# A streaming encoder step on one core: one weight sum moved between projections, a shorter sample softmax, other buffers for late gating, and a different order of the last split

## The chip, the cores and the metric

The kernel runs on one core of one Trainium2 chip. The metric is device time in microseconds (us) for one execution, as the median of the runs. The kernel before took 2306.07 us (three runs, 2305.02 to 2309.39). A measurement of this kernel can tell about 0.2% from no change.

## The reference, cut to what matters

One layer of a streaming encoder is applied to a prompt of 2048 tokens and to a batch of 8 samples with 16 tokens each, 2176 tokens in 17 tiles of 128. All arithmetic is float32.

```python
def trunk_layer(x, ...):                      # d_model 1024
    qm, km, vm, om, ip, fp, qa, ka, va = split_in(x @ w_in)         # in-projection
    hm = sigmoid(om) * head_norm(mlstm_chunkwise(qm, km, vm, ...))  # 4 heads x 128
    ha = swa(rope(qa), rope(ka), va, attn_sinks)                    # 8 query heads x 64, 2 kv heads
    mix = concat([hm, ha]) @ w_out                                  # out-projection
    h = layer_norm(alpha * x + mix)
    u = h @ w_up                                                    # 1024 -> 2 x 2816
    c = b_conv + sum(ext(u)[j:j + T] * w_conv[j] for j in range(3)) # causal depthwise
    a, g = split(c)
    return layer_norm(alpha * h + (silu(g) * a) @ w_down)           # 2816 -> 1024
```

The attention of the samples sees a cache of 128 keys and 16 new ones. Its softmax has a sink for each head, which counts in the maximum and in the sum:

```python
mx = maximum(max(s), sink)
p = exp(s - mx)
p = p / (sum(p) + exp(sink - mx))
```

## The kernel before

**Matrix products.** Every large product is float32 accuracy from reduced pieces: an operand is split into a high part (a cast on ScalarE, line 218) and a rest (a subtraction on VectorE, line 219), and three matmuls make one product (`mm3`, line 223, and the loops at 713, 1883 and 2090). The in-projection, the up-projection and the down-projection also use a scheme with seven products of half-size blocks in place of eight, for which sums of weight blocks and sums of token blocks are made on VectorE. The products are numbered 1 to 7 in the code (`s`).

**Buffers of weights.** Raw weights arrive by DMA in the seven buffers of tag `wraw` (`WR = 7`), 128 x 1024 float32 each, which all stages share. Their splits go to a ring of eight halves, later ten (tags `wlo`, `whi`, `wex`).

**Stages.** TensorE's order is the order of the program; the other engines' queues are put in order by the scheduler at compile time, which moves an operation ahead as soon as its inputs and its buffer allow.

1. In-projection (`i_dense`): four blocks of four prompt tiles (the samples go with block 0), five groups `g` of output columns, seven products each. Woven into it are chains for each tile (`t_sample`, `m_chain`, `a_chain`): the sample's mLSTM and attention (`swa_sample`, line 1480 on) and then the prompt's, tile by tile. A chain puts its matmuls between the dense ones at places that a plan with estimated costs sets.
2. Out-projection (`o_block`): five blocks of tiles, two halves `hf` of the output columns each, with the remaining chains woven in, and the first layer norm.
3. ConvFFN up (`f_ups`): three blocks of tokens (768, 768 and 640), 22 pairs of value and gate tiles each. `f_evict` copies TensorE's sums out, `f_after` does the convolution for the value (after product 3) and the gate (after product 4). For blocks 1 and 2, `f_gate` makes silu(gate) * value at once and stores it to `zf`. For block 0 the convolved tiles are stored to `zc` instead, and loaded back and gated later: 18 of them within block 1, four within block 2 (lines 1953 to 1959). The convolved tiles of the current pair and those that are loaded back share the two buffers of tag `cc`.
4. ConvFFN down (`f_downs`): three blocks, seven products, six units of weights each, with the second layer norm. `d_weights` loads and splits a unit; `pending` holds the norm steps of finished tiles (statistics, line 2128; two passes, lines 2130 and 2132), and `step` issues the next step of up to two of them. For the last block each step is put behind the latest split of weights on VectorE (`issue_after(self.low)`).

**Sums for the down-projection.** `d_sums` (line 849 on) makes ready the sums of `w_down` that stage 4 reads from `zt`, one pair of weight tiles k (of eleven) at a time. It has three steps: two loads of 512 KB, four subtractions of 128 x 512 on VectorE, two stores of 512 KB. Three of the eleven are made in the in-projection (line 691), in the single buffers `xr1` and `xr3`, and eight in the out-projection (line 1616), in two `wraw` buffers.

**From the out-projection to the ConvFFN.** The normed tiles come back from `zh` as `hst` (lines 1723 and 1725, on ScalarE's DMA queue), are transposed on TensorE (line 1707) between the matmuls of the last block of the out-projection, and the first ConvFFN weights (`wv`, `wg`, lines 1780 and 1782) are loaded meanwhile. The input of that last block comes as `xraw` from `zmix` and is split on ScalarE and VectorE (lines 902 to 907).

**Sample softmax.** In `swa_sample`, for each half of the batch: the maximum and a copy of the scores (lines 1511, 1512), the larger of the scaled maximum and the sink (1513), sink minus maximum (1514), its exponential (1515), the negated maximum (1516), four exponentials with sums (1518), sum and reciprocal (1519, 1520), and the scaling on GpSimd (1521). TensorE then transposes the result (1527, 1528).

Of the kernel before, what the change touches and what calls it, by code (L numbers as in the profile page):

```python
# [8 lines left out]
F32 = mybir.dt.float32  # L9
# [5 lines left out]
P = 128  # L15
# [190 lines left out]
class Prog:  # L206
# [384 lines left out]
    def i_dense(self):  # L591
# [36 lines left out]
        for item in self.items:  # L628
            if after:

                after[0] -= 1
                if after[0] == 3:
                    self.logs_of(after[1] - 1)
                if after[0] < 0:
                    self.i_done = after[1]
                    after = None
            self.chains.hold = item[0] == "t" and item[1] > 0
            if item[0] == "t":
                _, b, ti, e = item
                if ("g", e, 3) not in self.wu:  # L640
                    self.advance()
                if b not in self.gates:
                    self.gates[b] = self.tp.tile([P, 5, 8], F32, name="gates", tag="gates", bufs=2)
                if b == 0 and ti == 1:
                    for h in range(2):
                        for i in range(2):
                            yield from self.i_direct(b, i, e, self.ib[i * 2], (h,))
                    self.i_keys(b, 0, self.ib[0])
                    self.i_keys(b, 1, self.ib[2])
                    self.advance()  # L650
                    continue
                ps = self.bank([P, 512], "pg") if ti == 4 else self.ib[ti % 2 * 2]
                yield from self.i_direct(b, ti, e, ps)
                self.i_keys(b, ti, ps)
                if ti == 3 and b or ti == 4:
                    self.release(4)
                    self.x_steps(b, 4)
                    if b:
                        self.x_steps(b, 5)
                self.advance()  # L660
                continue
            _, b, g, s = item
            if item not in self.wu:
                self.advance()
            yield from self.i_product(b, g, s)
            del self.wu[item]
            self.release(2)
            if self.trans and s != 4:
                self.i_transposes()
            with self.tc.high_priority():  # L670
                behind = self.i_after(b, g, s)
            if (b, g, s) == (0, 0, 7):
                self.t_setup()
            if (g, s) == (last, 4):
                after = [8, b + 1]
            if g == last and b + 1 < nb:
                if s == 7:
                    for i in (0, 2):
                        self.rope_load(IBLOCKS[b + 1][i], 2)
                for x in passages[b > 0].get(s, ()):  # L680
                    if x == "load":
                        self.spare = True
                        self.x_load(b + 1, 1, 2, 3, 4)
                    else:
                        self.x_steps(b + 1, x)
            if g == last and b + 1 == nb and s in (7, 5, 2, 3):
                self.x_pair(0, (7, 5, 2, 3).index(s))
            with self.tc.issue_after(behind) if behind and b == 0 else nullcontext():
                self.advance()

            if (b, g) in ((nb - 2, 1), (nb - 1, 0), (nb - 1, 2)):

                steps = (6, 5, 3)
                if s in steps:
                    self.d_sums(sums, steps.index(s))
                    sums += s == steps[2]
# [244 lines left out]
    def t_setup(self):  # L941
        nc, a, tp = self.nc, self.a, self.tp

        def ld(n):
            t = self.one("k_" + n, list(a[n].shape))
            nc.sync.dma_start(t, a[n])
            return t
        nc.sync.dma_start(self.ident, a["ident"])
        self.gb = ld("gb")
        self.mcau = ld("mcau")  # L950
        self.mswa = ld("mswa")
        self.seg = ld("seg")
        self.sink = ld("sink")
        self.sinkx = ld("sinkx")
        self.m0 = ld("m0")
        self.nsink = self.one("nsink", [P, 8])
        nc.vector.tensor_scalar_mul(self.nsink, self.sink, -1.0)
        nc.vector.tensor_scalar_mul(self.sink, self.sink, 8.0)
        self.gm = ld("gm")
        nc.vector.tensor_scalar_mul(self.gm, self.gm, 0.5)  # L960

        raw = self.work("kw", [36, MH])
        nc.sync.dma_start(raw, a["sel"])
        self.sel = self.one("sel", [36, MH], F32R)
        nc.vector.tensor_copy(self.sel, raw)
        self.hl = [self.one(f"hl{i}", [36, P], F32R) for i in range(2)]
        self.ay = [self.one(f"ay{i}", [36, P]) for i in range(2)]
        for i in range(2):
            nc.vector.memset(self.ay[i], 0.0)
            nc.vector.tensor_copy(self.hl[i], self.ay[i])  # L970
        self.kh, self.kl = [self.one(n, [P, RING, P], F32R) for n in ("kringh", "kringl")]
        self.kv = {}
        self.C = self.work("C", [P, MH, 129], bufs=2)
        nc.vector.memset(self.C, 0.0)

        self.M = self.row("M")
        self.mc = self.M[:, P:]
        nc.vector.memset(self.mc, 0.0)
# [501 lines left out]
    def swa_sample(self, load, kvc):  # L1480
# [11 lines left out]
        mix = self.work("mixa", [P, 4, P])  # L1492
        NK = P + DS
        HB = DB // 2
        sk = self.sinkx.to_broadcast([P, HB])
        for half in range(2):
            bs = slice(half * HB, half * HB + HB)
            kc, vc = kvc
# [4 lines left out]
            for b0 in (0, 2):  # L1503
# [6 lines left out]
                        nc.tensor.matmul(ps[rs, i, P:], qs[rs, b], ks[rs, b * DS:(b + 1) * DS], start=True, stop=True)  # L1510
                V.tensor_reduce(mx[:, b0:b0 + 2], ps, axis=AX.X, op=ALU.max)
                V.tensor_copy(sc[:, b0:b0 + 2], ps)
            V.scalar_tensor_tensor(mx, mx, 0.125, sk, op0=ALU.mult, op1=ALU.max)
            V.tensor_sub(es, sk, mx)
            nc.scalar.activation(es, es, AF.Exp)
            V.tensor_scalar_mul(mx, mx, -1.0)
            for b in range(HB):
                nc.scalar.activation(sc[:, b], sc[:, b], AF.Exp, bias=mx[:, b:b + 1], scale=0.125, accum_out=sm[:, b:b + 1])
            V.tensor_add(sm, sm, es)
# [77 lines left out]
    def o_block(self, b):  # L1597
# [7 lines left out]
        for hf in range(2):  # L1605
            c = slice(hf * 512, hf * 512 + 512)
            steps = 0
            for cost, ti, ps in self.group(b, tiles, 8 * b + 4 * hf, hf == 1):
                yield cost
                if ps is None:  # L1610
                    steps += 1
                    if hf and b + 1 < nb and steps == 8 * len(tiles) - 6:
                        self.ynext = [self.o_x(t) for t in OBLOCKS[b + 1][:2]]
                    if steps % 2 == 0 and self.norms and next(self.norms[0], self) is self:
                        del self.norms[0]
                    if self.sums < NK2 and steps in (2, 18, 22):
                        self.d_sums(self.sums, (2, 18, 22).index(steps), True)
                        self.sums += steps == 22
                    continue
                y = outs[ti]  # L1620
                with self.tc.high_priority():
                    nc.vector.scalar_tensor_tensor(y[:, c], ys[ti][:, c], ALPHA, ps, op0=ALU.mult, op1=ALU.add)
                if hf and b == nb - 2 and ti >= len(tiles) - 2:

                    nc.sync.dma_start(self.zh[tiles[ti]], y)
                elif hf and b < nb - 1:
                    self.norms.append(self.norm(y, *self.ln1, self.zh[tiles[ti]]))
# [295 lines left out]
    def f_after(self, b, j, s):  # L1923
# [23 lines left out]
        if b == 0:  # L1947

            nc.sync.dma_start(self.zc[j], c)
            return  # L1950
        self.f_gate(c, b, j, WP, n)

        i = (b - 1) * NFF + j
        i = i if i < 18 else i - 6 if 24 <= i < 28 else None
        if b and i is not None:
            W0 = len(FBLOCKS[0]) * P
            c = self.f3.tile([P, 2, 768], F32, name="cc", tag="cc", bufs=2)[:, :, :W0]
            nc.sync.dma_start(c, self.zc[i])
            self.f_gate(c, 0, i, W0, W0)

    def f_gate(self, c, b, j, WP, n):
        nc, V = self.nc, self.nc.vector
        W = len(FBLOCKS[b]) * P
        th = self.f3.tile([P, 768], F32, name="th", tag="th", bufs=1)[:, :n]
        nc.scalar.activation(th, c[:, 1], AF.Tanh, scale=0.5)  # L1965
        V.scalar_tensor_tensor(th, th, 1.0, c[:, 1], op0=ALU.add, op1=ALU.mult)  # L1966
        V.tensor_mul(c[:, 0], th, c[:, 0])  # L1967
        nc.sync.dma_start(self.zf[b][j, :, :WP], c[:, 0, :WP])
        if n > WP:
            nc.sync.dma_start(self.zf[b][j, :, WP:].rearrange("p (b l) -> p b l", b=DB),  # L1970
                              c[:, 0, WP:].rearrange("p (b l) -> p b l", b=DB)[:, :, 2:])

# [88 lines left out]
    def f_downs(self):  # L2063
# [78 lines left out]
        for g, (b, s, u) in enumerate(self.dseq):  # L2142
# [41 lines left out]
                self.d_weights()  # L2184
            while self.nt < min(g + 6, len(self.dseq)):
                self.d_tokens()
            if b == nb - 1:
                with self.tc.issue_after(self.low):
                    step()


# [13 lines left out]
```

## Time and profile before

| | before |
|---|---|
| median of three runs | 2306.07 us |
| the profiled execution's own time | 2308.3 us |
| its span, first to last instruction | 2306.5 us |
| mean granted clock of TensorE | 0.998 |
| DVE (VectorE) busy | 1808.6 us, 78% |
| ACT (ScalarE) busy | 1271.4 us, 55% |
| POOL (GpSimd) busy | 273.7 us, 12% |
| DMA | 631.30 MB, 274 GB/s on average |

A row of the profile names the engine, the line of the kernel, the operation and its tiles (written<-read). PE is TensorE, PEld its weight loads, SPq the DMA queue of the Sync engine and ACTq that of ScalarE. What stands in square brackets is the idle time of the engine just before, and what ended it. Shares of DMA are of all 16 DMA engines of the core; they may come out slightly above 1.

### The profile page before, as it was taken

To read this page: it belongs to the slowest core of one execution; us is meant where nothing else is said; L and a number is where in the kernel's file an instruction comes from. 1 tells how busy PE (TensorE), PEld (TensorE's weight loads), DVE (VectorE), ACT (ScalarE), POOL (GpSimd) and SP (SyncE) were. 2 spreads that over 40 slices of the span, in tenths; PEclk is the share of its full clock that TensorE was granted. 3 is DMA by queue.
4 is the path that set the end of the run, shared out by engine and by line. 5 is a ranking of instruction groups with operands and counts; after the bars stand their busy time and mean duration, and the time that the engine had idled before them with its cause. 6 is when DMAs were issued, how large, how long until landed. Compare 5 with 4: busy or idle time off the path is not lost. (4 is left out here: it accounts for less than half of the span.)

```text
span 2306.5 us, 39717 instructions
## 1 busy us (share of the span) xinstructions
PE 2278.0 (99%) x14293; PEld 2092.2 (91%) x14293; DVE 1808.6 (78%) x3071; ACT 1271.4 (55%) x2373; POOL 273.7 (12%) x509
## 2 busy tenths in 40 slices
PE   9999999999999999999999999999999999999998
PEld 8999999999877777999999999999999978888876
DVE  8787587777688888998778777678766786895987
ACT  5453476776766655555656555555555544444442
POOL 0001001000121110211112100013111200100100
PEclk9999999999999999999999999999999999999999
DMA  7988898899997876898778888978998786757742
GB/s 279 322 306 291 296 315 276 276 305 299 326 327 257 280 246 250 304 325 302 276 277 277 303 302 312 311 255 288 308 299 261 246 297 214 253 172 222 255 155 83
DMA packets 299733, 631.30 MB, mean 274 GB/s; under 512 B 47820, under 2 KB 141072, under 8 KB 299536
## 3 DMA queue, kind: packets, MB, share of 16 engines
q1 hardware_dynamic: 294864, 615.06, 78.2%
q0 software_dynamic: 3520, 10.56, 1.5%
q10 hardware_dynamic: 1152, 3.15, 0.4%
q8 instruction: 113, 1.85, 0.3%
q14 instruction: 84, 0.69, 0.1%
HBM read 457.02 MB, written 171.64 MB: 273 GB/s over the span
## 5 line engine op out<-in xcount | busy, mean ns | idle before, releaser
L1883 PE MATMUL fup<-hh,uw 128*128 128x384 f32 (+1 forms) x1848 | 478.2, 328 | 1.2 <-ACT ua L1904 1.2
L1883 PE MATMUL dps<-hh,uw 128*128 128x384 f32 (+1 forms) x1848 | 477.8, 328 | 0.0
L1883 PEld LDWEIGHTS fup<-hh,uw 128*128 128x128 f32 x1848 | 330.1, 188 | 1.6 <-ACT ua L1904 1.5
L1883 PEld LDWEIGHTS dps<-hh,uw 128*128 128x128 f32 x1848 | 329.9, 188 | 0.0
L1941 DVE SCALAR_TENSOR_TENSOR cc<-u,cw,cc 128x768 f32<-128x768 f32 (+1 forms) x264 | 258.1, 978 | 63.2 <-ACT cc L1939 54.8
L1883 PE MATMUL fup<-hl,uw 128*128 128x384 f32 (+1 forms) x924 | 302.6, 327 | 1.0 <-DVE hl L219 1.0
L1883 PE MATMUL dps<-hl,uw 128*128 128x384 f32 (+1 forms) x924 | 302.4, 327 | 0.0
L713 PE MATMUL dps<-w,oh 128*128 128x256 f32 x1344 | 255.5, 285 | 0.0
L218 ACT CAST uw<-wraw 128x1024 fp32r<-128x1024 f32 x126 | 123.2, 978 | 230.2 <-PE dps L2090 122.2
L219 DVE TENSOR_TENSOR w<-wraw,w 128x1024 fp32r<-128x1024 f32 (+2 forms) x163 | 186.4, 1152 | 67.6 <-ACT w L218 61.6
L713 PEld LDWEIGHTS dps<-w,oh 128*128 128x128 f32 x1344 | 211.6, 189 | 11.1 <-issue 8.1
L218 ACT CAST w<-wraw 128x1024 fp32r<-128x1024 f32 (+2 forms) x163 | 160.0, 991 | 107.1 <-PE dps L713 55.4
L219 DVE TENSOR_TENSOR uw<-wraw,uw 128x1024 fp32r<-128x1024 f32 x126 | 142.2, 1129 | 62.9 <-ACT uw L218 62.0
L713 PE MATMUL dps<-w,ol 128*128 128x256 f32 x672 | 188.3, 280 | 0.0
L2090 PE MATMUL fup<-uw,fu 128*128 128x512 f32 x726 | 173.9, 396 | 1.6 <-ACT fht L2098 1.6
L1883 PEld LDWEIGHTS fup<-hl,uw 128*128 128x128 f32 x924 | 173.5, 188 | 1.7 <-DVE hl L219 1.6
L1883 PEld LDWEIGHTS dps<-hl,uw 128*128 128x128 f32 x924 | 173.5, 188 | 0.0
L713 PE MATMUL dps<-oh,w 128*128 128x256 f32 x896 | 168.0, 282 | 3.9 <-DVE w L219 2.3
L2090 PEld LDWEIGHTS fup<-uw,fu 128*128 128x128 f32 x726 | 136.3, 188 | 34.8 <-ACT fht L2098 2.0
L2090 PE MATMUL dps<-uw,fu 128*128 128x512 f32 x660 | 165.2, 396 | 1.1 <-DVE uw L219 1.1
L1939 ACT ACTIVATE cc<-u,cw 128x768 f32<-128x768 f32 (+1 forms) x132 | 132.1, 1001 | 48.7 <-DVE u L1921 23.4
L2090 PEld LDWEIGHTS dps<-uw,fu 128*128 128x128 f32 x660 | 123.9, 188 | 31.3 <-DVE uw L219 1.5
(318 smaller groups left out, 4574.1 us busy)
## 6 DMA issues: line engine op xcount, KB each, us to landing
uw<-zw SPq DMA_DIRECT2D x176, 512.0 KB, 5.2
zw<-uw SPq DMA_DIRECT2D x88, 512.0 KB, 3.5
w<-zws SPq DMA_DIRECT2D x72, 512.0 KB, 5.8
wv<-wup SPq DMA_DIRECT2D x66, 512.0 KB, 4.7
wraw<-wi SPq DMA_DIRECT2D x65, 512.0 KB, 5.1
wraw<-zt SPq DMA_DIRECT2D x60, 512.0 KB, 4.5
wraw<-wdn SPq DMA_DIRECT2D x45, 512.0 KB, 4.4
wraw<-wo SPq DMA_DIRECT2D x40, 512.0 KB, 5.4
```

The lines of the kernel that those rows point to most:

```text
L218: nc.scalar.copy(hi, src)
L219: return nc.vector.tensor_sub(lo, src, hi.bitcast(F32)).ins
L713: mm(o, l, r, start=s in (1, 7) and c == k == i == 0, stop=k == 3 and i == 2, skip_group_check=True)
L1883: mm(ps, l[:, k], r[:, k], start=s in (1, 7) and k == 0 and i == 0, stop=k == 3 and i == 2, skip_group_check=True)
L1939: S.activation(c[:, v], u[:, 2:2 + n], AF.Identity, bias=w[3], scale=w[2])
L1941: V.scalar_tensor_tensor(c[:, v], u[:, i:i + n], w[i], c[:, v], op0=ALU.mult, op1=ALU.add)
L2090: mm(ps, l[:, k, c], r[:, k], start=s in (1, 4, 7) and u == 0 and k == 0 and i == 0, stop=u == nu - 1 and k == n - 1 and i == 2, skip_grou ...
```

## The change

1. In the in-projection a fourth sum is made, in group 1 of the last block; in the out-projection the condition now allows sums up to the block and half `(nb - 2, 0)` only, so that seven are made there and none in the last half of the block before the last.
2. The sample softmax keeps the negated maximum from the start (`min` of -0.125 times the maximum and the negated sink), and the sink's exponential takes the sink as its bias. Lines 1514 and 1516 go; one operation that negates the sink is added at the setup of the chains.
3. The convolved tiles of block 0 are loaded back into two `wraw` buffers by two DMAs, gate first, and no longer into a `cc` buffer by one.
4. In the down-projection, the norm step that came between the last but one and the last split of weights is not issued there; what is pending is issued after the last unit.

```diff
@@ i_dense
-            if (b, g) in ((nb - 2, 1), (nb - 1, 0), (nb - 1, 2)):
+            if (b, g) in ((nb - 2, 1), (nb - 1, 0), (nb - 1, 1), (nb - 1, 2)):
@@ t_setup
+        self.nsinkx = self.one("nsinkx", [P, 1])
+        nc.vector.tensor_scalar_mul(self.nsinkx, self.sinkx, -1.0)
@@ swa_sample
-        sk = self.sinkx.to_broadcast([P, HB])
+        nsk = self.nsinkx.to_broadcast([P, HB])
...
-            V.scalar_tensor_tensor(mx, mx, 0.125, sk, op0=ALU.mult, op1=ALU.max)
-            V.tensor_sub(es, sk, mx)
-            nc.scalar.activation(es, es, AF.Exp)
-            V.tensor_scalar_mul(mx, mx, -1.0)
+            V.scalar_tensor_tensor(mx, mx, -0.125, nsk, op0=ALU.mult, op1=ALU.min)
+            nc.scalar.activation(es, mx, AF.Exp, bias=self.sinkx)
@@ o_block
-                    if self.sums < NK2 and steps in (2, 18, 22):
+                    if (b, hf) < (nb - 2, 1) and steps in (2, 18, 22):
@@ f_after
-        self.f_gate(c, b, j, WP, n)
+        self.f_gate([c[:, k] for k in range(2)], b, j, WP, n)
...
-            c = self.f3.tile([P, 2, 768], F32, name="cc", tag="cc", bufs=2)[:, :, :W0]
-            nc.sync.dma_start(c, self.zc[i])
+            c = [self.wp.tile([P, 768], F32, name="cz", tag="wraw", bufs=WR)[:, :W0] for _ in range(2)]
+            for k in (1, 0):
+                nc.sync.dma_start(c[k], self.zc[i][:, k])
             self.f_gate(c, 0, i, W0, W0)
@@ f_downs
-            if b == nb - 1:
+            if b == nb - 1 and self.nw != len(self.dseq) - 1:
                 with self.tc.issue_after(self.low):
                     step()
+        while pending:
+            step()
```

In `f_gate` the indices `c[:, 0]` and `c[:, 1]` become `c[0]` and `c[1]`, with the same operations.

More of the change, by code (lines that the diff above doesn't have):

```diff
@@ L1964, in f_gate @@
         th = self.f3.tile([P, 768], F32, name="th", tag="th", bufs=1)[:, :n]
[L1965 to L1968, printed above, removed]
+        nc.scalar.activation(th, c[1], AF.Tanh, scale=0.5)
+        V.scalar_tensor_tensor(th, th, 1.0, c[1], op0=ALU.add, op1=ALU.mult)
+        V.tensor_mul(c[0], th, c[0])
+        nc.sync.dma_start(self.zf[b][j, :, :WP], c[0][:, :WP])
         if n > WP:
             nc.sync.dma_start(self.zf[b][j, :, WP:].rearrange("p (b l) -> p b l", b=DB),
-                              c[:, 0, WP:].rearrange("p (b l) -> p b l", b=DB)[:, :, 2:])
+                              c[0][:, WP:].rearrange("p (b l) -> p b l", b=DB)[:, :, 2:])
     def d_begin(self):
```

## The prediction

> **What bounds the kernel now.** First the page's busy times, then the list of waits of TensorE, longest first (microseconds in all, times, longest).
>
> ```profile
> PE 2278.0 (99%) x14293; PEld 2092.2 (91%) x14293; DVE 1808.6 (78%) x3071; ACT 1271.4 (55%) x2373; POOL 273.7 (12%) x509
> ...
> PE fht L1707 <- DMA hst<-zh: 4.3, 3, 3.1
> PE ppt L1527 <- POOL v L1103: 2.9, 1, 2.9
> ...
> PE fup L2090 <- ACT fht L2098: 1.6, 1, 1.6
> ...
> PE fup L1883 <- ACT ua L1904: 1.2, 1, 1.2
> PE dps L2090 <- DVE uw L219: 1.1, 1, 1.1
> ```
>
> TensorE is busy for 2278.0 of 2306.5 us, and the change takes no matmul away. What it can win are the waits in this list, and four of its parts each stand beside one: the batch's softmax (2.9, the POOL row), the last transposes ahead of the ConvFFN (4.3), the gating (1.2), the last split (1.1). Together these are 9.5 us.
>
> A wait can cost more than its gap. The busy times in windows show the granted clock (third number from the end; the last two are DMA share and GB/s) after the two longest single waits, and after the one of 1.6 us:
>
> ```profile
> 254.00:258.00 4.00, 4.00 (x23) 3.92 (x22) 0.00 (x0) 1.82 (x3) 0.00 (x0) 0.59 0.59 168
> 882.00:886.00 4.00, 4.00 (x17) 3.55 (x18) 2.35 (x2) 1.41 (x3) 0.00 (x0) 0.58 0.11 45
> 1858.00:1860.00 2.00, 1.91 (x8) 1.60 (x9) 1.50 (x2) 2.00 (x5) 0.00 (x0) 1.00 1.04 394
> ```
>
> TensorE counts as busy in both first windows, but at 0.59 and 0.58 of its clock: 4 us times 0.41 or 0.42 is 1.65 us of work lost, twice. After the wait of 1.6 us the clock was 1.00. So I count that a stall that falls below 1.6 us takes 1.65 us of slow clock with it. [...] The trace has the fall behind both stalls.
>
> **The change part by part.** *The batch's softmax.* Its first half in order of time (start, length, engine, line):
>
> ```profile
> 246.67 0.15 DVE L1513 SCALAR_TENSOR_TENSOR amx<-amx,k_sinkx 128x4 f32<-128x4 f32 x1
> ...
> 248.55 1.22 DVE L219 TENSOR_TENSOR w<-wraw,w 128x1024 fp32r<-128x1024 f32 x1
> ...
> 249.69 0.16 DVE L1516 TENSOR_SCALAR amx<-amx 128x4 f32<-128x4 f32 x1
> 249.88 0.41 ACT L1518 ACTIVATE scs<-scs,amx 128x144 f32<-128x144 f32 x1 [1.01 <-DVE amx L1516]
> ...
> 251.61 0.17 DVE L1519 TENSOR_TENSOR asm<-asm,aes 128x4 f32<-128x4 f32 x1 [1.77 <-ACT scs L1518]
> ...
> 252.13 1.15 POOL L1521 TENSOR_TENSOR scs<-scs,asm 128x576 f32<-128x576 f32 x1 [26.37 <-DVE asm L1520]
> ...
> 253.34 0.33 PE L1527 MATMUL ppt<-ident,scs 128*128 128x128 f32 x1 [2.85 <-POOL v L1103]
> ```
>
> The operations of lines 1514 and 1516 go. What counts is not their 0.16 us each but that VectorE does other work ahead of each, the split of 1.22 us among it: ScalarE's exponentials start at 249.88, 3 us after the minimum is there (246.82). Without them the exponentials can start near 247; the four took 1.73 us (249.88 to 251.61), so even behind another operation of ScalarE they are done before VectorE leaves its split at 249.77. The sum of line 1519 then runs there and not at 251.61: 1.9 us earlier, and with it the chain behind it; I take 2.0. The stall falls from 2.85 to about 0.9, and the slow clock goes: **3.6 us**. Bounds: 0 (the schedule keeps the old spacing) and 2.85 + 1.65 = 4.5. The second half has no wait in the list: nothing. The new negated sink is one more operation like that of line 1516, early, where no wait of TensorE is left to lengthen by more than its 0.16 us: nothing.
>
> *One sum less in the out-projection.* Its four subtractions on VectorE delay nobody in the list. Its transfers do (rows of the engines, then two windows):
>
> ```profile
> 849.12 0.33 SPq L865 DMA_DIRECT2D zt<-txy  x1
> ...
> 866.68 0.33 SPq L1780 DMA_DIRECT2D wv<-wup  x1
> ...
> 867.53 0.62 ACT L906 CAST oh<-xraw 128x512 fp32r<-128x512 f32 x1 [2.44 <-DMA xraw<-zmix]
> ...
> 870.67 0.34 ACTq L1725 DMA_DIRECT2D hst<-zh  x1
> ...
> 881.91 1.94 PE L1707 MATMUL fht<-ident,hst 128*128 128x128 f32 x8 [3.09 <-DMA hst<-zh]
> ...
> 850.00:866.00 16.00, 16.00 (x70) 12.14 (x69) 11.12 (x17) 4.87 (x9) 2.90 (x2) 1.00 0.99 332
> 866.00:882.00 16.00, 11.70 (x60) 8.90 (x60) 8.79 (x11) 7.46 (x10) 0.00 (x0) 1.00 1.04 416
> ```
>
> From 850 to 882 the DMA engines are full (shares 0.99 and 1.04). The last load of hst leaves ScalarE's queue at 870.67 and is waited for until 881.91; the loads ahead of it were queued on ScalarE behind casts that themselves waited for transfers, like the one at 867.53. The two stores of the sum, 1.05 MB, are 3.2 us of the full stretch at 332 GB/s and 2.5 at 416. I take 3.0, as they stand in its first half: of 4.3 us of waiting 1.3 stay, under the 1.6 that left the clock alone, so the 1.65 go too: **4.6 us**. Bounds: 0 and 4.3 + 1.65 = 5.9.
>
> *The fourth sum in the in-projection* uses the third one's two single buffers after it (SP's queue, TensorE, one window, one row of the page's issues):
>
> ```profile
> 485.06 0.96 SPq L854 DMA_DIRECT2D txy<-wdn  x1
> ...
> 504.21 0.41 SPq L866 DMA_DIRECT2D zt<-txy  x1
> ...
> 523.27 2.18 SPq L483 DMA_DIRECT2D w<-zws  x3
> ...
> 532.46 0.28 PE L713 MATMUL dps<-w,oh 128*128 128x256 f32 x1
> ...
> 510.00:530.00 20.00, 20.00 (x168) 17.46 (x167) 11.37 (x48) 14.75 (x41) 2.01 (x4) 1.00 1.03 351
> ...
> w<-zws SPq DMA_DIRECT2D x72, 512.0 KB, 5.8
> ```
>
> The third runs from 485 to 504, so the fourth would run from about 509 to 528, and there the DMA engines are full (1.03). The stored half that is issued at 523.27 lands some 5.8 us later, at 529.1; the product that starts at 532.46 has 3.4 us in hand. Loads and stores of one sum are 2.1 MB, at 351 GB/s 6.0 us. If all of that goes ahead of these halves, on SP's queue or in the engines, TensorE waits 2.6 us and with the clock 4.3; if only the loads do, it does not wait. There is no wait of TensorE here to gain. I take a third of the bare wait: **-0.9 us**.
>
> *Later gating in raw buffers.* The 1.25 us, what ScalarE (which issues in order) waited for ahead of it, the same wait over the whole run, one product, and the load of a raw weight:
>
> ```profile
> 1637.35 0.85 ACT L1965 ACTIVATE th<-cc 128x768 f32<-128x768 f32 x1 [4.12 <-DMA cc<-zc]
> ...
> 1641.30 0.93 ACT L1939 ACTIVATE cc<-u,cw 128x656 f32<-128x656 f32 x1 [1.69 <-DMA zf<-cc]
> ...
> 1642.59 0.41 PE L1883 MATMUL fup<-hh,uw 128*128 128x320 f32 x1 [1.25 <-ACT ua L1904]
> ...
> ACT cc L1939 <- DMA zf<-cc: 22.5, 21, 2.0
> ...
> 1664.00 1.76 PE dps L1883 x12
> ...
> wv<-wup SPq DMA_DIRECT2D x66, 512.0 KB, 4.7
> ```
>
> With cc's two buffers kept for the current tile, neither wait is left. In exchange each pair of tiles takes four turns of the seven raw buffers, not two. Taken in turn, a load of wv gets its buffer when the last split of the wg two pairs earlier ends, three products (5.3 us at 1.76) ahead of its own split; the earlier split's own 1.2 us (as long as the one at 248.55) off, 4.1 us are left for a load of 4.7. ScalarE would wait about 0.6 us per pair, where it now waits 22.5 / 21 = 1.1 us for the stores mostly unnoticed. The 22 more DMA issues fall to SP, 0.33 us each like that at 849.12, between loads made long ahead; without that cover they would be 7 us. I take **0.9 us** of the 1.25. Bounds: 1.25, and below nothing the third rival.
>
> *Last split ahead of a norm step.*
>
> ```profile
> 2282.45 2.47 DVE L2130 SCALAR_TENSOR_TENSOR yacc<-yacc,lmv,f_ln_g 128x1024 f32<-128x1024 f32 x2
> ...
> 2284.84 0.68 DVE L219 TENSOR_TENSOR uw<-wraw,uw 128x512 fp32r<-128x512 f32 x1
> ...
> 2285.58 0.74 PE L2090 MATMUL dps<-uw,fu 128*128 128x512 f32 x2 [1.09 <-DVE uw L219]
> ...
> 2298.93 0.69 DVE L2119 SCALAR_TENSOR_TENSOR yacc<-yacc,fht 128x512 f32<-128x512 f32 x1 [1.25 <-PE fht L2090]
> ```
>
> The split would run from 2282.45 to 2283.13, before TensorE asks at 2284.49. The norm steps come 0.68 us later; VectorE still waits for TensorE at 2298.93, so the end moves with TensorE: **1.1 us**. Bound: 0, if another operation slips in.
>
> **The sum:** 3.6 + 4.6 - 0.9 + 0.9 + 1.1 = 9.3 us. The profiled execution took 2308.3 us, 1.8 of them outside its span; it would take 2299.0. It lies 2.2 above the median of the runs, 2306.07, so the median becomes **2296.8**.
>
> **The rivals.**
> 1. *Prefetch takes what the stores free.* The two raw buffers of the sum go to the ConvFFN's first weights: the load at 866.68 comes earlier, and the next pair of loads takes its place beside hst. For: the engines are full up to 882, whoever fills them. Against: the first pair then goes ahead of the full stretch. The hst term is gone: 2306.07 - 4.7 = 2301.4. [...] 0.17.
> 2. *The fourth sum stalls the in-projection* at 532: 4.3 lost and not 0.9 gives 2300.2. For: 3.4 us in hand against 6.0. Against: the third sum moved as much and stalled nobody in the list. 0.10.
> 3. *Slower: the raw ring.* If loads of wv hold ScalarE as long as it was held at 1637 and 1641 (4.12 + 1.69 = 5.8 us) at each of the 22 gates, each costs TensorE 1.25: 27.5 us, less the other parts' 8.4, gives 2325. It decides from a landing of 4.1 + 5.8 = 9.9 us on; the median is 4.7. 0.07.
> 4. *The clock falls although the stalls are short:* 3.3 us stay, 2300.1. 0.06.
> 5. *The change does not do what it says:* VectorE's order keeps the softmax as late as before; 3.6 us stay, 2300.4. 0.05.
> 6. Two of the smaller ones together: about 2305. 0.05.
>
> **How the numbers follow.** The forecast has 0.50. A measurement of this kernel can tell about 0.2%, 4.6 us, from no change: faster is below 2301.5, slower above 2310.7. Faster: 0.47 of the forecast, half of rival 1, most of 2, 4 and 5, in all 0.70. Slower: rival 3, 0.07. Within: the rest, 0.23. The low end takes the upper bounds, 4.5 + 5.9 + 1.25 + 1.1 = 12.75: 2293. The high end takes in rivals 1, 2, 4 and 5 with some spread: 2304; left out are rivals 3 and 6 and the tails.
>
> **What would show it.** In the list of waits: the POOL row of ppt at 1 us or less, hst under 2, no row for ua or for the last uw; a granted clock of 1.00 near 254 and 882; no wait near 532; ScalarE's waits for wv under 1 us each. An unchanged 3 us at hst, or a new wait of TensorE above 1.6 us anywhere, would make the prediction wrong.

## The result, and the profile after

The changed kernel takes 2302.03 us (median of 16 runs, 2299.82 to 2305.87), the kernel before on the same chip 2307.43 (16 runs). The ratio is 0.998, 95% interval 0.9973 to 0.9986: 5.4 us faster, where 9.3 were forecast. The profiled execution took 2301.44 us with a span of 2299.7, 6.8 less than the span before.

From the list of waits of TensorE of the changed kernel:

```profile
PE ppt L1354 <- ACT pth L1355: 2.7, 1, 2.7
...
PE ppt L1527 <- POOL scs L1521: 0.8, 1, 0.8
PE ppt L1354 <- DVE C L1235: 0.8, 1, 0.8
```

The rows for hst, ua and the last uw are gone, and the row of the samples' softmax fell from 2.9 to 0.8. At the top stands a wait that the kernel before did not have: the transposes of line 1354, in the attention chain of the in-projection.

Where the time went can be read from landmarks, because both kernels run the same 14293 matmuls in the same order. These rows are starts of the same TensorE work: the transposes of four chains' gates (pcol, called a to d below), the first product of the ConvFFN (line 1883), and the last products (fht). First the kernel before:

```profile
305.25 0.25 PE L1034 MATMUL pcol<-ident,ay 36*128 36x36 f32 x1
...
484.18 0.25 PE L1034 MATMUL pcol<-ident,ay 36*128 36x36 f32 x1
518.39 0.25 PE L1034 MATMUL pcol<-ident,ay 36*128 36x36 f32 x1
818.96 0.25 PE L1034 MATMUL pcol<-ident,ay 36*128 36x36 f32 x1
903.47 0.34 PE L1883 MATMUL fup<-hh,uw 128*128 128x384 f32 x1
...
2286.16 12.73 PE L2090 MATMUL fht<-uw,fu 128*128 128x512 f32 x54
```

Then the changed kernel:

```profile
301.97 0.25 PE L1036 MATMUL pcol<-ident,ay 36*128 36x36 f32 x1
...
480.98 0.25 PE L1036 MATMUL pcol<-ident,ay 36*128 36x36 f32 x1
520.12 0.25 PE L1036 MATMUL pcol<-ident,ay 36*128 36x36 f32 x1
821.12 0.25 PE L1036 MATMUL pcol<-ident,ay 36*128 36x36 f32 x1
899.10 0.34 PE L1883 MATMUL fup<-hh,uw 128*128 128x384 f32 x1
...
2278.55 12.73 PE L2091 MATMUL fht<-uw,fu 128*128 128x512 f32 x54
```

| stretch | holds | before | after | difference |
|---|---|---|---|---|
| start to a | softmax of the samples | 305.25 | 301.97 | -3.3 |
| b to c | the sums in the in-projection | 34.21 | 39.14 | **+4.9** |
| d to line 1883 | the end of the out-projection | 84.51 | 77.98 | **-6.5** |
| line 1883 to fht | gating, last split | 1382.69 | 1379.45 | -3.2 |
| fht to the end of the span | tail | 20.3 | 21.1 | +0.8 |

The stretches left out add 0.5; all of it gives the 6.8 of the spans. Two windows of the changed kernel answer to those of before (length, TensorE busy, granted clock, DMA share, GB/s), and a third lies behind the new wait:

```profile
254.00:258.00 4.00, 4.00 (x49) 1.00 0.96 333
...
882.00:886.00 4.00, 4.00 (x28) 1.00 0.79 268
...
514.29:517.70 3.41, 3.41 (x11) 0.50 0.79 272
```

Where the two old stalls stood the clock is full; behind the new one it is half for 3.41 us, 1.7 us lost beside the waits of 0.80 and 2.66.

The new stall begins on SP's queue, where the loads of a sum wait for stores of the sum before (waits between 480 and 520 us):

```profile
SPq L855 <- DMA zt<-txy: 3.5, 1, 3.5
SPq L854 <- DMA zt<-txy: 2.6, 1, 2.6
```

Its way on, in order of time, through SP, VectorE, ScalarE, POOL and TensorE (in brackets the idle time before and what ended it):

```profile
498.34 0.33 SPq L854 DMA_DIRECT2D txy<-wdn  x1
...
503.93 0.69 DVE L860 TENSOR_TENSOR txy<-txy 128x512 f32<-128x512 f32 x1 [3.79 <-DMA txy<-wdn]
505.12 0.17 ACT L1165 ACTIVATE mr<-pnum 128x2 f32<-128x2 f32 x1 [3.78 <-DVE bmv L1163]
...
509.85 2.50 POOL L1172 TENSOR_TENSOR ms<-mr,mhalf 128x4 f32<-128x4 f32 x1 [9.58 <-DVE mr L1171]
...
512.38 1.28 ACT L1178 ACTIVATE hn<-hn,ms 128x128 f32<-128x128 f32 x4 [2.32 <-POOL ms L1172]
513.56 1.04 ACT L1355 COPY pth<-ppt 128x512 f32<-128x512 f32 x2
...
514.18 1.06 PE L1354 MATMUL ppt<-ident,sc 128*128 128x128 f32 x4 [2.66 <-ACT pth L1355]
```

The added sum and the one after it share xr1 and xr3 with the sum before. Each load waits until the store before it has landed, so the first load of the last sum (k = 3) is issued at 498.34 only. The compiler had placed that sum's first subtraction ahead of bn_stats (the statistics of the head norm) of the mLSTM chain on VectorE. VectorE stands there for 3.79 us, and bn_stats, behind that subtraction in its queue, start at 504.54 only (at 501.77 in the run below that leaves the subtractions out). Behind that come mr on ScalarE, ms on POOL, hn on ScalarE, and behind hn in ScalarE's queue the copies of the attention's transposes, for which TensorE waits.

In the kernel before, line 860 of the last sum waited less, and 12 us ahead of the chain's bn_stats (504.00):

```profile
491.69 0.69 DVE L860 TENSOR_TENSOR txy<-txy 128x512 f32<-128x512 f32 x1 [2.47 <-DMA txy<-wdn]
```

### The profile page after: what moved, and what is told of

It is laid out like the page before. It is cut to its first block, busy times and chain, and to the rows that moved or that the text cites. A ratio compares the mean times of both kernels' runs of the same rounds, so it can differ in the third digit from the quotient of the medians.

```text
span 2299.7 us, 39828 instructions
## 1 busy us (share of the span) xinstructions
PE 2275.3 (99%) x14293; PEld 2090.5 (91%) x14293; DVE 1810.8 (79%) x3068; ACT 1272.3 (55%) x2373; POOL 277.5 (12%) x509
## 4 chain that ended last, share of the span: by engine, by line
PE 84%; DVE 2%; DMA 2%; issue 0%; ACT 0%; POOL 0%; SPq 0%; DVEq 0%; POOLq 0%; ACTq 0%
PE dps L1883 20%; PE fup L1883 20%; PE dps L713 9%; PE dps L2091 7%; PE fup L2091 6%; PE fht L2091 6%; PE dps L223 3%; PE dps L225 2%; PE dps L224 2%; PE ppo L1360 1%; PE psc L1315 1%; PE ppt L1354 1%; PE dps L739 1%; PE fht L1707 1%; PE pscore L1140 1%; PE pnum L1223 1%
## 5 line engine op out<-in xcount | busy, mean ns | idle before, releaser
L1883 PE MATMUL fup<-hl,uw 128*128 128x384 f32 (+1 forms) x924 | 302.9, 328 | 0.9 <-DVE hl L219 0.9
L713 PEld LDWEIGHTS dps<-oh,w 128*128 128x128 f32 x896 | 140.0, 188 | 9.6 <-issue 4.9
```

Of the source, the lines that this page charges most:

```text
L713: mm(o, l, r, start=s in (1, 7) and c == k == i == 0, stop=k == 3 and i == 2, skip_group_check=True)
L1883: mm(ps, l[:, k], r[:, k], start=s in (1, 7) and k == 0 and i == 0, stop=k == 3 and i == 2, skip_group_check=True)
```

## The experiments

Two theories on the new stall. **A:** the place on VectorE; who stands in its queue behind a subtraction that waits for a late load. **B:** the 2.1 MB of more traffic in a stretch where the DMA engines are full. Own times below are those of the profiled execution (2301.44 for the changed kernel); ratios are against the kernel before, run on the same chip. All of their intervals but the last overlap with that of the changed kernel (0.9973 to 0.9986), so the readings rest on rows and landmarks of the traces; each is one execution.

**Other buffers for the added sum.**

```diff
-            self.txy = x, y = [p.tile([P, D], F32, name="txy", tag=tag, bufs=n) for p, tag, n in (pool(1), pool(3))]
+            self.txy = x, y = [p.tile([P, D], F32, name="txy", tag=tag, bufs=n) for p, tag, n in (pool(1 + (k == 2)), pool(3 + (k == 2)))]
```

> The third sum of the in-projection (k = 2, the added one) uses the buffers xr2 and xr4, so that no load of a sum waits for the stores of the sum just before it; bytes, number of sums and their places in the program are those of the changed kernel. Theory A (VectorE waits in order at line 860 for a load that waited for the store of the sum before; the mLSTM chain stands behind it): the wait of 3.79 us at line 860 near 504 goes or falls under 1 us, TensorE's waits of 0.80 us at 506 and 2.66 us at 514 go, its clock stays 1.00 between 510 and 520, and the profiled execution is about 4.5 us under the changed kernel's 2301.4, at 2296.9 (2296 to 2299). Theory B (the 2.1 MB more traffic in a full stretch): the same bytes move in the same stretch, the stall stays or moves by a few us, and the time stays within 1.5 us of 2301.4.

Ratio 0.9974 (0.9965 to 0.9984), 2299.14 us; own time 2298.69. Half of it: 35.03 us from b to c, 4.1 less than the changed kernel, and no slow clock (1.00 from 505 to 525), but a wait of VectorE and one of TensorE stay:

```profile
502.22 0.69 DVE L861 TENSOR_TENSOR txy<-txy 128x512 f32<-128x512 f32 x1 [2.91 <-DMA txy<-wdn]
...
508.15 2.50 POOL L1172 TENSOR_TENSOR ms<-mr,mhalf 128x4 f32<-128x4 f32 x1 [7.17 <-DVE mr L1171]
...
512.47 0.66 PE L1354 MATMUL ppt<-ident,sc 128*128 128x128 f32 x4 [1.49 <-ACT pth L1355]
```

The traffic is the same and the stall is nearly halved, which B did not give. A's place is confirmed, its size was not: the waits were to go, but the second load of the last sum is still late for line 861.

**No subtractions in the last sum.**

```diff
+        if step == 1 and k == 3: return
         if step == 1:
```

> Leaves out the four subtractions of the last sum made in the in-projection (k = 3, whose first one waits near 504); its two loads and two stores stay, in the same order on SP's queue, so that the sum stored for k = 3 is the raw weights. Theory A: with no subtraction on VectorE that waits, bn_stats and what follows run about 3.8 us earlier, the waits at 506 and 514 and the slow clock after them go, and the profiled execution is about 4.5 us under the changed kernel's 2301.4, at 2296.9. Theory B: the traffic is the same, so the stall of 2.66 us stays, and the time with it (2301.4 less at most 0.5).

Ratio 0.9964 (0.9950 to 0.9977), 2297.24 us; own time 2297.80. The rows of POOL and TensorE, and a window of five us:

```profile
508.30 1.04 POOL L1172 TENSOR_TENSOR ms<-mr,mhalf 128x4 f32<-128x4 f32 x1 [6.31 <-DVE mr L1171]
...
511.47 1.03 PE L1354 MATMUL ppt<-ident,sc 128*128 128x128 f32 x8
```

```profile
510.00:515.00 5.00, 5.00 (x40) 1.00 1.09 368
```

TensorE waits for nothing there and its clock is full, while the DMA engines are full too (1.09): all bytes of the sum move and the stall is gone. **B falls** as what stalls TensorE; how far full DMA engines make the loads themselves land late is not shown. The rows also split the delay. Here hn starts at 509.38, 2.09 us ahead of TensorE's transposes at 511.47; in the changed kernel it starts 1.46 behind them (512.38 against 510.92), 3.55 later in all. Of these, 2.1 come from VectorE (line 1171 runs at 508.00, 3.47 ahead of the transposes, and at 509.55, 1.37 ahead, in the changed kernel), and 1.46 from POOL, whose operation ms takes 2.50 and not 1.04. The copies of pth had 0.9 us in hand (510.57 to 511.47), so TensorE waits 3.55 - 0.9 = 2.65: the 2.66 of the row. With the added sum in other buffers, the same arithmetic gives 2.38 - 0.9 = 1.48, against 1.49 in its row.

**The sums undone in the changed kernel.** 
```diff
-            if (b, g) in ((nb - 2, 1), (nb - 1, 0), (nb - 1, 1), (nb - 1, 2)):
+            if (b, g) in ((nb - 2, 1), (nb - 1, 0), (nb - 1, 2)):
...
-                    if (b, hf) < (nb - 2, 1) and steps in (2, 18, 22):
+                    if self.sums < NK2 and steps in (2, 18, 22):
```

> The changed kernel with part 1 undone: three sums in the in-projection, eight in the out-projection. If the forecast's mechanism of the hst wait holds (the eighth sum holds raw buffers and queues ahead of the last block of the out-projection), TensorE's waits for hst (4.3 us in all, and the slow clock, 1.65 us) come back near 880, and the in-projection loses the waits at 506 and 514: the two cancel, 2301.4 + 5.3 - 4.7 = 2302.0 for the profiled execution. Rival C (the hst waits went because of another part of the change, which shifted everything by 3 us): they stay away, and the time falls by the in-projection's 4.7 us to about 2296.7.

Ratio 0.9985 (0.9976 to 0.9994), 2302.92 us; own time 2301.11. The waits of the in-projection go (33.77 us from b to c) and those for hst come back (a row of the waits, then landmark d and line 1883):

```profile
PE fht L1707 <- DMA hst<-zh: 3.6, 2, 2.9
```

```profile
815.56 0.25 PE L1036 MATMUL pcol<-ident,ay 36*128 36x36 f32 x1
897.49 0.34 PE L1883 MATMUL fup<-hh,uw 128*128 128x384 f32 x1
```

From d to line 1883 it takes 81.93 us, 4.0 more than the changed kernel, so it was the sum in the out-projection that made the wait, and rival C falls. It is 2.6 less than before (84.51): the wait is 3.6 and not 4.3, and the clock stayed full behind it (1.00 from 870 to 890). As a whole, part 1 is worth too little for the timed runs to show.

**The sums alone in the kernel before.** The diff of the experiment before, the other way round, and nothing else changed.

> The kernel before with part 1 alone: four sums in the in-projection, seven in the out-projection. Theory A with the forecast's mechanism for the out-projection: minus 5.0 us near 880 (waits for hst and the slow clock), plus 4.9 us near 506 to 520, so that the time is that of the kernel before within 1 us (2308.3 for the profiled execution). The forecast's own sum for this part was minus 3.7 us (2304.6). Near 252 the softmax's wait of 2.85 us stays; the slow clock after it (1.65 us) may come or not, since a wait of the same length came without it in the run with the softmax undone.

Ratio 0.9994 (0.9985 to 1.0002), 2304.55 us; own time 2305.95.

```profile
484.90 0.25 PE L1034 MATMUL pcol<-ident,ay 36*128 36x36 f32 x1
...
523.78 0.25 PE L1034 MATMUL pcol<-ident,ay 36*128 36x36 f32 x1
824.95 0.25 PE L1034 MATMUL pcol<-ident,ay 36*128 36x36 f32 x1
902.98 0.34 PE L1883 MATMUL fup<-hh,uw 128*128 128x384 f32 x1
```

38.88 us from b to c (+4.7) and 78.03 at the end of the out-projection (-6.5), with 0.6 more between them: -1.2 by the landmarks, and no difference in the timed runs. So also without the other three parts, part 1 loses in the one place most of what it wins in the other.

**The softmax undone in the changed kernel.** 
```diff
...
-            V.scalar_tensor_tensor(mx, mx, -0.125, nsk, op0=ALU.mult, op1=ALU.min)
-            nc.scalar.activation(es, mx, AF.Exp, bias=self.sinkx)
+            V.scalar_tensor_tensor(mx, mx, 0.125, sk, op0=ALU.mult, op1=ALU.max)
+            V.tensor_sub(es, sk, mx)
+            nc.scalar.activation(es, es, AF.Exp)
+            V.tensor_scalar_mul(mx, mx, -1.0)
```

> The changed kernel with the former softmax of the samples. By the forecast's step: TensorE's wait of 2.85 us near 252 and the slow clock after it come back, 3.3 to 3.6 us, so that the profiled execution is at 2304.7 to 2305.0 against the changed kernel's 2301.4. Rival (the softmax chain is covered, and the gain near 252 was of something else): no more than 0.5 us.

Ratio 0.9991 (0.9982 to 1.0000), 2303.62 us; own time 2301.48. The wait is back to the hundredth, the slow clock is not (a row of TensorE, then windows of 3.41 us):

```profile
253.07 0.33 PE L1527 MATMUL ppt<-ident,scs 128*128 128x128 f32 x1 [2.85 <-POOL v L1103]
```

```profile
248.41:251.82 3.41, 1.80 (x16) 1.00 0.89 278
251.82:255.24 3.42, 2.17 (x19) 1.00 0.86 301
...
514.65:518.06 3.41, 3.41 (x12) 0.50 0.67 239
```

So the wait's 2.0 us are the softmax's (2.85 against 0.84 in the changed kernel), and the 1.65 of slow clock are not in every execution. The execution as a whole was not the 3.3 us longer that were expected: it is 1.5 us behind the changed kernel at landmark a (303.45), and has made that up at c (520.02), in stretches that the edit does not touch.

**The last split undone in the changed kernel.** 
```diff
-            if b == nb - 1 and self.nw != len(self.dseq) - 1:
+            if b == nb - 1:
...
-        while pending:
-            step()
```

> The changed kernel with part 4 undone (the last norm step is again put behind the last but one split). By the forecast's step TensorE's wait before the last products comes back (about 1.1 us near 2270); by the trace of the changed kernel its tail, from the last matmul to the end, is 0.77 us longer than before (8.40 against 7.63), because one pass of the tile before (line 1553, 0.75 us) now stands between the last product's sum (line 2120) and the last statistics. So the whole is 1.2 - 0.8 = 0.4 us slower than the changed kernel, with a tail of 7.6. Rival: the tail is longer for another reason and stays 8.4; then it is 1.2 us slower.

Ratio 0.9986 (0.9977 to 0.9995), 2303.11 us; own time 2302.27, 0.8 more than the changed kernel's. The wait of 1.1 us for uw is back, and the tail from fht to the end is 20.6 us and not 21.1. The tail of the changed kernel shows why (VectorE):

```profile
2291.31 0.69 DVE L2120 SCALAR_TENSOR_TENSOR yacc<-yacc,fht 128x512 f32<-128x512 f32 x1 [0.58 <-PE fht L2091]
2291.92 0.75 DVE L1553 SCALAR_TENSOR_TENSOR yacc<-yacc,lsc,f_ln_b 128x512 f32<-128x512 f32 x1
2292.58 0.69 DVE L1565 BATCH_NORM_STATS2 st<-yacc 128x6 f32<-128x512 f32 x1
```

VectorE waits for the last product, then runs a pass of the tile before (line 1553), and only then the last statistics. The reading of the expectation holds, with 0.5 us for its 0.8: from line 1883 (899.54) to fht (2279.89) it takes 0.9 more than the changed kernel, less the 0.5 gives the 0.4 expected. The other 0.4 of the 0.8 lie ahead of line 1883, where the edit changes nothing.

**The gating undone in the changed kernel.** 
```diff
...
-            c = [self.wp.tile([P, 768], F32, name="cz", tag="wraw", bufs=WR)[:, :W0] for _ in range(2)]
-            for k in (1, 0):
-                nc.sync.dma_start(c[k], self.zc[i][:, k])
+            c = self.f3.tile([P, 2, 768], F32, name="cc", tag="cc", bufs=2)[:, :, :W0]
+            nc.sync.dma_start(c, self.zc[i])
```

> The changed kernel with part 3 undone (the convolved tiles come back into the buffers of tag cc). By the forecast's step ScalarE's wait of 2 us for a cc buffer and TensorE's stall near 1640 come back: 1.4 to 1.5 us slower than the changed kernel (2302.9 for the profiled execution). Rival (the stall near 1640 went because all was shifted): within 0.3 us of it.

Ratio 0.9983 (0.9975 to 0.9992), 2301.93 us; own time 2304.64. In the timed runs it does not differ from the changed kernel. In its trace the stall is back, larger than before:

```profile
PE fup L1883 <- ACT ua L1904: 1.7, 1, 1.7
```

From line 1883 (900.84) to fht (2281.96) it takes 1381.12 us, 1.7 more than the changed kernel. (Another 1.5 us lie between landmarks a and b, 180.55 us and not 179.01, in work that the edit does not touch.) The wait varies: the trace of the sums alone, which has the former gating too, waited only 0.18 us at ua, where ScalarE's wait for the load into cc was 2.41 us and not 4.12. No trace with the new gating has a wait for ua there. The mechanism is shown, its size in the time is not.

**The last sum's subtractions late.**

```diff
...
-                    self.d_sums(sums, steps.index(s))
+                    with self.tc.issue_after(self.wlow) if s == 5 and sums == 3 else nullcontext(): self.d_sums(sums, steps.index(s))
```

Here wlow is the latest split of weights on VectorE.

> The changed kernel, all of its work done, with the four subtractions of the last sum of the in-projection (k = 3) issued on VectorE behind the latest split of weights, some 40 us later, where their loads have long landed. Theory A (VectorE's in-order queue stands behind the first subtraction): as in the run that leaves them out, no wait at line 860 near 504, no stall of TensorE at 506 and 514, clock 1.00 from 505 to 525, about 4.5 us under the changed kernel: profiled execution 2296.9 (2296 to 2299). Theory B (traffic): no change, 2301. A third possibility: the buffers xr1 and xr3 come free later, the two loads for the out-projection that take them come later too, and what is won at 514 is lost near the begin of the out-projection (a wait of TensorE for ScalarE or VectorE near 690 to 720).

Ratio 0.9970 (0.9960 to 0.9980), 2299.65 us; own time 2300.38. The stall at 514 is gone (33.31 us from b to c), and the third possibility came in, at 648 and not at 690 to 720 (ScalarE, POOL, TensorE):

```profile
637.47 1.05 ACT L906 CAST oh<-xraw 128x1024 fp32r<-128x1024 f32 x1 [2.91 <-DMA xraw<-zmix]
...
641.85 4.16 POOL L1172 TENSOR_TENSOR ms<-mr,mhalf 128x4 f32<-128x4 f32 x1 [6.69 <-DVE mr L1171]
...
647.85 0.66 PE L1354 MATMUL ppt<-ident,sc 128*128 128x128 f32 x4 [2.67 <-ACT pth L1355]
```

The buffers come free later (the stores of the sum are issued from 555.00 on and not from 512.42), xraw is loaded later, and now a cast on ScalarE waits for it with the chain's mr queued behind. It is the same kind of stall by another engine: from c to d it takes 304.74 us (515.15 to 819.89), 3.7 more than in the changed kernel. Some 2.3 us of the delay are in POOL's row: that operation took 1.90 us at this place in the changed kernel.

**The last sum in other buffers.** 
```diff
-            self.txy = x, y = [p.tile([P, D], F32, name="txy", tag=tag, bufs=n) for p, tag, n in (pool(1), pool(3))]
+            self.txy = x, y = [p.tile([P, D], F32, name="txy", tag=tag, bufs=n) for p, tag, n in (pool(1 + (k == 3)), pool(3 + (k == 3)))]
```

> The changed kernel, all of its work done, with the last sum of the in-projection (k = 3) in xr2 and xr4, so that its loads wait for no store of a sum, and stand earlier on SP's queue; the compiler then puts all of the four subtractions ahead of the chain's bn_stats on VectorE. (With the added sum k = 2 there instead, a wait of 2.9 us at line 861 was left, and a stall of 1.5 us.) Theory A: no wait over 1 us of VectorE for a load of weights between 480 and 505, no stall of TensorE between 500 and 520, no new one near 600 as with the late subtractions, and a time as with the subtractions left out: profiled execution 2296.5 to 2298, ratio to the kernel before 0.996 to 0.997. Theory B (traffic): a stall of about 2.7 us somewhere between 500 and 620 stays.

Ratio 0.9967 (0.9955 to 0.9979), 2296.80 us; own time 2296.35. A load of the last sum, and then the first subtraction of the added one:

```profile
464.04 0.43 SPq L854 DMA_DIRECT2D txy<-wdn  x1
...
493.08 0.69 DVE L860 TENSOR_TENSOR txy<-txy 128x512 f32<-128x512 f32 x1 [1.13 <-DMA txy<-wdn]
```

The loads of the last sum now wait for no store: they are issued at 464.04 and 469.84, ahead of the stores of the sum before (475.73 and 480.77), and its subtractions end near 482. It has passed the added sum, which stays in xr1 and xr3 behind those stores: its loads are issued at 485.43 and 488.53, and VectorE waits for them 1.13 and 0.58 us (slightly over the 1 us expected). But that is early enough: VectorE then has work without a gap up to the chain's bn_stats at 501.10. From b to c it takes 33.32 us, 0.9 less than before the change, and from d to line 1883 still 78.05. With that, part 1 is worth what was won at 880.

**The same, and the last pass ahead of the last sum.** The edit of the experiment before, and:

```diff
-            V.scalar_tensor_tensor(y[:, c], y[:, c], s[:, 0:1], bb[:, c], op0=ALU.mult, op1=ALU.add)
+            self.tail = V.scalar_tensor_tensor(y[:, c], y[:, c], s[:, 0:1], bb[:, c], op0=ALU.mult, op1=ALU.add).ins
...
-            with self.tc.high_priority():
+            with self.tc.issue_after(self.tail) if t == last_tile and hasattr(self, "tail") else self.tc.high_priority():
```

> The kernel with the last sum in xr2 and xr4, and in the tail the last product's sum (line 2120) issued behind the last pass of the tile before it (line 1553), which stood between that sum and the last statistics. By the reading of the tail: VectorE idles 0.58 us ahead of that sum anyway, the pass of 0.75 us fits in it, and the tail from the last matmul to the end falls from 8.4 to 7.7 us: 0.6 to 0.7 us less than the same kernel without it. Rival (the tail is set by the stores of the tile before): no change.

Ratio **0.9959** (0.9946 to 0.9971), 2295.27 us, the lowest of all, though its interval overlaps with that of the run before; own time 2298.64. The tail, from fht (2276.26) to the end (2296.8), is 20.5 us and not 21.1, as expected. Its profiled execution is the slower one all the same: from line 1883 to fht it takes 1382.32 us, 3.1 more than in the run before. Of these, 1.6 are a wait for ScalarE at the first products of the down-projection (line 2099, 2.7 us against 1.1), at a place that the edit does not touch and that varies from run to run (0.4 to 2.7 us in the traces that list it); where the rest went is not shown.

## Why the prediction was right or wrong

- **What bounds the kernel: right.** Nearly all that was won lies at the four waits that were named.
- **The softmax: right.** 3.6 us forecast, 3.3 measured at landmark a. The 1.65 us of slow clock in it was certain for no execution: with the former softmax in the changed kernel the same 2.85 us cost no clock.
- **One sum less in the out-projection: mechanism right, size too small in this pair of traces.** 4.6 forecast, 3.0 of it waiting; 6.5 measured. The wait for hst did not fall from 4.3 to 1.3 but went altogether. With this part undone in the changed kernel it was 4.0, because 3.6 us of waiting cost no clock there. That the surplus here made up for part of the loss in the next point is luck. Rival 1 (prefetch takes what the stores free) did not come: the load of wv that was issued at 866.68, ahead of the last four loads of hst, is now issued at 871.15, behind the last one (870.91).
- **The fourth sum in the in-projection: the step that failed.** The forecast was -0.9, "a third of the bare wait", at 532, from bytes and the stored halves of the weights. Measured: -4.9 at 506 to 520, and no wait at 532. The five traces with the added sum in xr1 and xr3 and all its subtractions in their place (the changed kernel and four of the experiments) take 37.6 to 39.1 us from b to c, 3.4 to 4.9 more than before, each with slow matmuls behind the stall: the four of ppo (line 1360, in two of them 1358) took 1.44 to 1.98 us, and 1.08 behind the stall of the late subtractions. I counted whose transfers the sum delays and left out what stands on VectorE behind its first subtraction. The trace before had the row: line 860 already waited 2.47 us at 491.69 for its load. The argument "the third sum moved as much and stalled nobody" compared bytes, and the harm is in the order. Rival 2 had the price (4.3) but the wrong place and cause. The forecast's own sign, a new wait above 1.6 us, came in here with 2.66.
- **The gating: right in sign, 1.5 measured against 0.9** (matmul for matmul, the changed kernel is 4.4 us ahead at 1600 and 5.9 at 1660). ScalarE now waits 16.7 us for wv, 8 times, 3.9 at the longest, where under 1 us each was said; none of it reached TensorE. The third rival's waits came in part, its price did not. The 1.5 belong to this pair of traces: with the former gating the wait was 0.2 to 1.7 us long.
- **The last split: 1.4 us at TensorE against 1.1 (6.2 us ahead at 2250, 7.6 at the last products), less 0.8 in the tail.** "The end moves with TensorE" was wrong: the norm steps that were pushed back put one pass of 0.75 us between the last product and the last statistics.
- **Rivals 4 and 5 did not come:** the clock was full at both old places, and the softmax came earlier.

The sum by the trace: 3.3 - 4.9 + 6.5 + 3.2 - 0.8 - 0.5 = 6.8 against 9.3, and 5.4 (3.2 to 6.2) in the timed runs.

## What to carry to other kernels

The added sum cost here what was queued behind one operation that waited for a transfer: 3.79 us on VectorE, with bn_stats behind it, became 2.66 us at TensorE, and the compiler had placed that operation ahead of the chain's. So look first at the wait in an added operation's row and at the next instructions of its engine, then at its bytes. Work that repeats in single buffers had its loads wait for the stores before them (2.6 and 3.5 us on SP's queue). In the traces here, a second pair of buffers for the last sum removed the stall, while moving the subtractions in time moved it to the next user of the buffers; the ratios (0.9967 and 0.9970) do not tell the two apart. When a queue is reordered ahead of a deadline, follow the displaced steps to the end of the program.

## What the runs showed of the hardware

**In these traces the half clock lies on a grid of 3.413 us, and the length of a stall alone does not tell whether it comes.** In the trace before, the two stretches of half clock amid the work are 3.413 us long and begin at 253.86 and 881.91: 628.05 us apart, 184 times 3.413 to within 0.1. One more begins at 2301.86, behind the last matmul, 2048.00 us behind the first (600 times 3.4133). In the changed kernel half clock begins at 514.29 and, behind the last matmul, at 2296.05: 1781.76 us apart, 522 times 3.4133. Cut into windows of that length, each trace has half clock behind a window in which TensorE was hardly busy (in the changed kernel 0.75 us, from 510.88):

```profile
250.45:253.86 3.41, 0.56 (x6) 1.00 0.88 320
253.86:257.27 3.41, 3.41 (x19) 0.50 0.56 164
...
878.50:881.91 3.41, 0.32 (x2) 1.00 1.03 420
881.91:885.33 3.42, 3.42 (x13) 0.50 0.16 66
```

In the run with the softmax undone half clock begins at 514.65; counted back from there, 77 windows, one begins at 251.82. If the grid holds there too, the stall of 2.85 us was cut in two: 1.80 and 2.17 us of either window stayed busy, and the clock stayed full (1.00). The forecast's "a stall that falls below 1.6 us takes 1.65 us of slow clock with it" held where the windows lay as in the trace before. How little work in a window goes with half clock stays open: it followed windows with 0.32 to 1.96 us busy (the 1.96 without the last sum's subtractions, from 331.08), and full clock followed some with as little as 1.81 (before, from 1854.71). In that run without the subtractions the clock was half from 334.50 to 337.91, where the edit touches nothing, and the stretch from a to b takes 180.5 us and not 179.0. It takes as long with the split undone and with the gating undone, where the clock in that stretch is not shown. Landmark a varies too: in four experiments (the two with the last pair, the two pairs, the late subtractions) it lies at 302.9 and not at 302.0, and with the sums alone 0.8 later than before; the cause is not shown. Differences of that size between two traces say nothing of an edit unless they lie at its place.

**A small operation of GpSimd took longer in some places where VectorE was busy beside it.** The 128x4 operation of line 1172 took 1.04 us without the sum's subtractions, 2.50 where they follow VectorE's split, and 4.16 where VectorE ran three splits and a sum without a gap. In the kernel before (line 1170 there) six of its 17 had VectorE idle beside them and took 1.05 us; the other eleven took 1.03 to 2.49, and one of them, at 677.35, took 1.05 with VectorE busy throughout. No run changed only what VectorE does beside it, so the 1.46 us are read from the rows, and that VectorE causes them is not shown by an experiment.
